# Dilated attention in a two-layer trunk: queries ordered by residue mod 4, two head groups in one contraction

## The chip, the cores and the metric

One Trainium2 chip, one of its cores. The metric is device time in microseconds for one execution of the whole program; smaller is better. TensorE is called PE here (PEld is its weight load), VectorE is DVE, ScalarE is ACT, GpSimd is POOL, and SP is the engine that issues most transfers.

## What is computed

Two layers over 256 tokens of width 1024, all in 32-bit floats. In each layer 24 heads of width 64 get q, k and v. Twelve of them are dilated heads, in three groups of four; six use plain causal softmax and six use stick-breaking attention. The part that matters:

```python
DIL_GROUPS = ((128, 1), (512, 4), (2048, 16))
# Query t attends to t, t-d, t-2d, ..., t-(window/d)*d. Returns (out, logsumexp)

def dilated_mixture(q, k, v):
    outs, lses = [], []
    for g, (w, d) in enumerate(DIL_GROUPS):
        sl = slice(g * HEADS_PER_DIL_GROUP, (g + 1) * HEADS_PER_DIL_GROUP)
        o, lse = dilated_window_attention(q[:, sl], k[:, sl], v[:, sl], w, d)
        outs.append(o)
        lses.append(lse)
    o = jnp.stack(outs, axis=0)
    wgt = jax.nn.softmax(jnp.stack(lses, axis=0), axis=0)
    return jnp.sum(wgt[..., None] * o, axis=0)
```

Weighting by the softmax of the log-sums is the same as one softmax over the keys of all three groups, and so the kernel computes it. With 256 tokens a query of group 1 meets keys at distances 0, 4, 8, ..., one of group 2 at 0, 16, 32, ...: in both cases only keys with its own residue mod 4, 64 of the 256. Around attention stand the projections (q, k, v, gates), the output projections with sigmoid gates, and a squared-ReLU MLP.

## The kernel before, in words

Activations lie with features on partitions and tokens along the free axis (`xres`, 128x8x256). Weights come in 280 pieces of 128x1024 (512 KB) in the order of use, through 4 buffers `raw`; SP issues every load (L109). Each piece is split by ACT (`wh`, L128) and DVE (`wl`, L129) into a high and a low part, in 6 buffers each, and a projection is three products per 128 rows (L211 to L213) of a 128x128 weight tile with 256 tokens. PE holds the weight tile, loaded by its own instruction before each product.

A layer begins with v for all heads (`v_chunk`, three chunks of 8 heads, L287), written out by `v_out` (L256) into `V[c]`, with tokens on partitions, as high and low parts. Then `MIX_ORDER` alternates q/k pairs (`qk_pair`, two heads each), gate tiles and attention units: `run_units` takes one or two units after each projection. A scheduler then orders the instructions of each engine by data dependence and priority, so that attention instructions stand between projection products in PE's queue.

`att_softmax(fs, kt_out, units)` does two dilated heads of each of the three groups (a "pair": `fs` names one q/k pair per group), twice per layer, four times in the program. `softmax_first` (L370) makes scores for the first 128 queries, `softmax_second` (L380) those for the other 128 against all 256 keys: 6 products of 64 rows (one head's width; the two heads j=0 and j=1 lie in the two halves of the rows) by 128 keys, and 6 by 256. `burst` (L312) keeps them together in PE's queue. The scores are plain 32-bit products, and each of them runs as two PE instructions (the trace has 192 of L319 for 96 in the program). `softmax_rows` (L349) adds the mask, takes the maximum, the exponential and the division, over 384 or 768 columns a head. `values(j)` (L409) then transposes the probabilities, three 128x128 tiles per group (L413 to L415), splits each result into `ph` and `pl`, and multiplies with V (`pv_mm`, L346 with both parts of V, 128 columns wide, and L347 with the high part, 64 wide). The same function with one group (G = 1) serves the six plain heads. `o_head` (L330) adds the two halves of the result.

Of the kernel before, what the change touches and what calls it, by code (L numbers as in the profile page):

```python
# [15 lines left out]
P = 128  # L16
# [28 lines left out]
NORM_ACT = False  # L45
TAIL = 4
# [17 lines left out]
def trunk(ctx: ExitStack, tc: tile.TileContext, w, x, norms, gfin, consts, out):  # L64
# [159 lines left out]

    hl = hilo_slot(0)
# [4 lines left out]
    for layer in range(DEPTH):  # L230
# [33 lines left out]

        def v_chunk(c, n):
# [23 lines left out]
            if c > 0:  # L289
                v_out(c)  # L290
# [21 lines left out]
        def burst(jobs, after=None):  # L312

            before = None
            with tc.high_priority(offset=BPRI):
                for dst, f, j, qs, ks, flipped, first in jobs:
                    t, own = QK[f], slice(j * DH, j * DH + DH)
                    q, k = t[own, 0, qs], t[own, 1, ks]
                    i = pe.matmul(dst, k if flipped else q, q if flipped else k, start=first, stop=True, skip_group_check=True)  # L319
                    if before is None and after is not None:  # L320
                        tc.add_manual_dep(i.ins, after.ins.name, READ, reason="the banks are free together")
                    if before is not None:
                        tc.add_manual_dep(i.ins, before.ins.name, QUEUED, reason="one burst of scores")
                    before = i

# [4 lines left out]
        def o_head(po, oF, j):  # L330

            tmp = T("tmp", [DH, S], 2)
            act.activation(tmp, po[DH:P, 0:S], AF.Copy)
            dve.tensor_tensor(oF[j * DH:(j + 1) * DH], po[0:DH, 0:S], tmp, op=ALU.add)
# [5 lines left out]
        def pv_mm(po, head, kt, ph, pl, first, last):  # L340

            c, s = divmod(head, 8)
# [19 lines left out]
        def att_softmax(fs, kt_out, units):  # L362

            G = len(fs)
            p0 = {}
            p1 = {}
            env = {}
            mA = cst["maskA"] if G == 3 else cst["maskB"].unsqueeze(1)

            def softmax_first():  # L370

                s0 = s_bank()
                t0 = T("wk", [P, 2, 3, P], WK)
                burst([(s0[:, j, g * P:(g + 1) * P], fs[g], j, T0, T0, False, True) for g in (2, 1, 0) for j in range(2)])
                for j in range(2):
                    env["read"] = softmax_rows(t0[:, j], s0[:, j, 0:384].rearrange("p (a b) -> p a b", a=3),
                                 mA[:, :, T1], env["den"][:, j:j + 1])
                    p0[j] = t0[:, j]

            def softmax_second():  # L380

                s1 = [s_bank().rearrange("p a b -> p (a b)") for _ in range(2)]
                burst([(s1[j][:, g * S:(g + 1) * S], fs[g], j, T1, TT, False, True) for g in (2, 1, 0) for j in range(2)], env["read"])
                for j in range(2):
                    t1 = T("wk", [P, 3, S], WK)
                    softmax_rows(t1, s1[j][:, 0:768].rearrange("p (a b) -> p a b", a=3), mA, env["den"][:, 2 + j:3 + j])
                    p1[j] = t1

            def softmax_one():
                s1 = s_bank()  # L390
                t1 = T("wk", [P, 2, 384], WK)
                burst([(s1[:, j, 0:S], fs[0], j, T1, TT, False, True) for j in range(2)]
                      + [(s1[:, j, S:384], fs[0], j, T0, T0, False, True) for j in range(2)])
                for j in range(2):
                    softmax_rows(t1[:, j, 0:S], s1[:, j, 0:S], cst["maskB"], env["den"][:, j:j + 1])
                    softmax_rows(t1[:, j, S:384], s1[:, j, S:384], cst["maskB"][:, T1], env["den"][:, 2 + j:3 + j])
                    p1[j] = t1[:, j:j + 1, 0:S]
                    p0[j] = t1[:, j:j + 1, S:384]

            def score():  # L400
                env["den"] = T("den", [P, 4], 3)
                if G == 3:
                    softmax_first()
                else:
                    softmax_one()
# [3 lines left out]
            def values(j):  # L409
                po = t_bank()  # L410
                for g in range(G):
                    tb = t_bank()
                    pe.transpose(tb[:, 0:P], p0[j][:, g], ident)  # L413
                    pe.transpose(tb[:, P:2 * P], p1[j][:, g, T0], ident)
                    pe.transpose(tb[:, 2 * P:3 * P], p1[j][:, g, T1], ident)  # L415
                    ph = T("ph", [P, 384], 2, F32R)
                    pl = T("pl", [P, 384], 2, F32R)
                    act.activation(ph, tb[:, 0:384], AF.Copy)
                    dve.tensor_tensor(pl, tb[:, 0:384], ph.bitcast(F32), op=ALU.subtract)
                    head = 2 * fs[g] + j  # L420
                    pv_mm(po, head, 0, ph[:, 0:S], pl[:, 0:S], g == 0, False)
                    pv_mm(po, head, 1, ph[:, S:384], pl[:, S:384], False, g == G - 1)
# [3 lines left out]

            units += [score] + [softmax_second] * (G == 3) + [lambda: values(0), lambda: values(1)]

# [350 lines left out]
```

## Time and profile before

| | us |
|---|---|
| median of 3 runs (869.42 to 870.21) | 870.13 |
| the profiled execution's own time | 869.13 |
| its span | 867.4 |
| PE busy | 855.4 (99%) |
| PEld busy | 780.6 (90%) |
| DVE busy | 638.3 (74%) |
| ACT busy | 475.5 (55%) |

Busy times overlap: a product's record reaches from its issue to its end and the next one starts inside it, so PE's 99% says that PE is hardly ever without work, and not how fast it works. What an instruction costs PE is read from the distance between the starts of neighbours. PE's granted clock is 0.999 over the span, that is 2.4 GHz throughout but for the start.

### The profile page before, as it was taken

What the parts mean: (1) busy time and instruction counts of PE and PEld (TensorE: products, weight loads), DVE (VectorE), ACT (ScalarE), POOL (GpSimd) and SP (SyncE); (2) the same over time, 40 slices, a digit from 0 to 9 for tenths busy, and PEclk for the clock granted to TensorE, in tenths of its full rate; (3) what the DMA queues carried; (4) which work ended last, traced back from release to release, by engine and by line L of the source; (5) the groups of instructions that cost most, each with busy time, mean ns of one, the idle gap of its engine ahead of it and who ended that gap; (6) DMA issues with size and microseconds to landing.
All of it is one profiled execution on the core that took longest, in us unless ns stands there. A gap on an engine that the chain in (4) does not pass through costs nothing.

```text
span 867.4 us, 14607 instructions
## 1 busy us (share of the span) xinstructions
PE 855.4 (99%) x5776; PEld 780.6 (90%) x5776; DVE 638.3 (74%) x962; ACT 475.5 (55%) x685; POOL 23.9 (3%) x36
## 2 busy tenths in 40 slices
PE   8999999999999999999999999999999999999996
PEld 6899999999998888888888999999999988888885
DVE  6978878855977766666578878798568977666664
ACT  6756666758454544444465665666574545444442
POOL 0000101000000000000000101010000000000000
PEclk9999999999999999999999999999999999999999
DMA  8854534454666565665555554435555675666641
GB/s 311 270 169 150 165 126 144 147 171 135 185 209 199 178 189 192 194 195 187 177 174 166 172 162 135 141 124 165 168 158 166 220 210 180 192 193 192 184 136 48
DMA packets 42835, 151.36 MB, mean 175 GB/s; under 512 B 4880, under 2 KB 5264, under 8 KB 42768
## 3 DMA queue, kind: packets, MB, share of 16 engines
q1 hardware_dynamic: 42336, 149.90, 54.8%
q8 instruction: 45, 0.74, 0.3%
q10 hardware_dynamic: 432, 0.54, 0.2%
q14 instruction: 22, 0.18, 0.1%
HBM read 149.37 MB, written 1.05 MB: 173 GB/s over the span
## 4 chain that ended last, share of the span: by engine, by line
PE 93%; DVE 2%; ACT 2%; issue 1%; DMA 1%; SPq 0%; POOLq 0%; DVEq 0%; ACTq 0%
PE mm L219 14%; PE mm L211 11%; PE mm L212 11%; PE mm L213 10%; PE mm L222 7%; PE s L603 7%; PE s L604 7%; PE s L605 7%; PE s L287 5%; PE s L319 2%; PE mm L287 2%; PE s L211 1%; PE t L346 1%; PE s L212 1%; PE s L213 1%
## 5 line engine op out<-in xcount | busy, mean ns | idle before, releaser
L129 DVE TENSOR_TENSOR wl<-raw,wh 128x1024 fp32r<-128x1024 f32 (+1 forms) x281 | 342.0, 1220 | 111.9 <-ACT wh L128 111.4
L128 ACT ACTIVATE wh<-raw 128x1024 fp32r<-128x1024 f32 (+1 forms) x281 | 294.8, 1053 | 221.2 <-PE mm L219 77.0
L211 PE MATMUL mm<-hl,wl 128*128 128x256 f32 x832 | 234.2, 282 | 0.0
L212 PE MATMUL mm<-hl,wh 128*128 128x256 f32 x832 | 233.1, 281 | 0.0
L213 PE MATMUL mm<-hl,wh 128*128 128x256 f32 x832 | 232.5, 280 | 0.6 <-DVE hl L242 0.4
L211 PEld LDWEIGHTS mm<-hl,wl 128*128 128x128 f32 x832 | 156.3, 188 | 0.8
L213 PEld LDWEIGHTS mm<-hl,wh 128*128 128x128 f32 x832 | 155.9, 188 | 1.0 <-DVE hl L242 1.0
L212 PEld LDWEIGHTS mm<-hl,wh 128*128 128x128 f32 x832 | 156.2, 188 | 0.3
L219 PE MATMUL mm<-hl,wh 128*128 128x512 f32 x512 | 129.1, 392 | 0.3 <-DVE wk L575 0.3
L219 PEld LDWEIGHTS mm<-hl,wh 128*128 128x128 f32 x512 | 93.7, 188 | 18.4 <-DVE wk L575 0.5
L603 PE MATMUL s<-wl,ga 128*128 128x512 f32 x256 | 100.4, 392 | 0.0
L604 PE MATMUL s<-wh,ga 128*128 128x512 f32 x256 | 100.0, 391 | 0.0
L605 PE MATMUL s<-wh,ga 128*128 128x512 f32 x256 | 99.0, 389 | 0.0
L222 PEld LDWEIGHTS mm<-hl,wl 128*128 128x128 f32 x512 | 70.4, 190 | 5.2
L575 DVE TENSOR_REDUCE wk<-mm 128x256 f32<-128x512 f32 x64 | 44.1, 691 | 41.4 <-PE mm L222 41.3
L222 PE MATMUL mm<-hl,wl 128*128 128x256 f32 x512 | 72.0, 282 | 0.0
L605 PEld LDWEIGHTS s<-wh,ga 128*128 128x128 f32 x256 | 48.0, 188 | 10.2
L603 PEld LDWEIGHTS s<-wl,ga 128*128 128x128 f32 x256 | 48.2, 188 | 9.9 <-ACT wk L668 0.5
L580 ACT ACTIVATE ga<-wk 128x512 fp32r<-128x512 f32 x32 | 20.2, 631 | 66.1 <-DVE wk L577 66.1
L604 PEld LDWEIGHTS s<-wh,ga 128*128 128x128 f32 x256 | 48.2, 188 | 8.8
L211 PE MATMUL s<-hl,wl 128*128 128x256 f32 x128 | 36.0, 281 | 0.6 <-DVE wk L531 0.6
L212 PE MATMUL s<-hl,wh 128*128 128x256 f32 x128 | 35.6, 278 | 0.0
(128 smaller groups left out, 1041.4 us busy)
## 6 DMA issues: line engine op xcount, KB each, us to landing
raw<-in_w_dram SPq DMA_DIRECT2D x279, 512.0 KB, 3.6
xres<-in_x_dram SPq DMA_DIRECT2D x4, 256.0 KB, 5.7
raw<-in_w_dram SPq DMA_DIRECT2D x2, 256.0 KB, 4.2
wk<-in_gfin_dram SPq DMA_DIRECT2D x2, 256.0 KB, 4.0
out_dram<-V SPq DMA_DIRECT2D x2, 256.0 KB, 2.3
out_dram<-V ACTq DMA_DIRECT2D x2, 256.0 KB, 2.1
c_maskA<-in_maskA_dram SPq DMA_DIRECT2D x1, 384.0 KB, 6.8
c_rope<-in_rope_dram SPq DMA_DIRECT2D x1, 256.0 KB, 6.6
```

Of the source, the lines that this page charges most:

```text
L128: act.activation(hi[:, c:c + step], r[:, c:c + step], AF.Copy)
L129: dve.tensor_tensor(lo[:, c:c + step], r[:, c:c + step], hi[:, c:c + step].bitcast(F32), op=ALU.subtract)
L211: pe.matmul(dst, lo[:, c:c + P], hl[:, koff + k, 0], start=a, stop=False, skip_group_check=True)
L212: pe.matmul(dst, hi[:, c:c + P], hl[:, koff + k, 0], start=False, stop=False, skip_group_check=True)
L213: pe.matmul(dst, hi[:, c:c + P], hl[:, koff + k, 1], start=False, stop=z, skip_group_check=True)
L219: pe.matmul(bank, hi[:, k * P:k * P + P], hl[:, k].rearrange("p a b -> p (a b)"), start=k == 0, stop=False, skip_group_check=True)
L222: pe.matmul(bank[:, 0:S], lo[:, k * P:k * P + P], hl[:, k, 0], start=False, stop=k == KT - 1, skip_group_check=True)
L287: last_mm = pe.matmul(pv[t], xs[:, k, x_part, t * P:t * P + P], w_part[:, wsl], start=k == 0 and w_part is hi and x_part == 0, stop=k == K ...
L575: dve.tensor_reduce(t[:, a], p[a].rearrange("p (a b) -> p b a", a=2), axis=mybir.AxisListType.X, op=ALU.add)
L603: pe.matmul(dst, uh[:, j % 2, k], lo[:, c], start=j == 0, stop=False)
L604: pe.matmul(dst, uh[:, j % 2, k], hi[:, c], start=False, stop=False)
L605: return pe.matmul(dst, ul[:, j % 2, k], hi[:, c], start=False, stop=j == 2 * npairs - 1)
```

## The change

The tokens of a query half are put on the score partitions by residue: partition r*32+i holds query 4i+r of the half. For the groups 1 and 2 a product then takes only the 32 queries and the 64 keys of one residue, and writes its own 32 partitions. Group 0 has the same order of queries, so it too is cut into four products of 32 queries, against 128 or 256 keys. Both halves become one softmax row layout of 256 or 384 columns a head (it was 384 or 768), with new masks. `att_softmax` is left for the plain heads.

For the contraction with V the probabilities of groups 1 and 2 lie side by side (64 + 64 columns), so one transpose serves both, and one product per residue contracts over 128 partitions: 64 keys of group 1 and 64 of group 2. V of those heads must lie that way, by residue: the chunks of v are reordered (`V_HEADS`) so that chunk 1 holds just these eight heads, and `v_out_dilated` writes it to four tiles `y` (in the buffers `ga`) and moves it by 16 transfers per layer, from SP, into `V[1]`.

```diff
+V_HEADS = list(range(0, 4)) + list(range(12, 16)) + list(range(4, 12)) + list(range(16, 24))
...
+        def v_out_dilated(c):
+
+            rcol, pv = factors["rcol"], banks[c]
+            V[c] = T("V", [P, DIL, 4, 2, DH], 3, F32R)
+            for t in range(2):
+                for g in range(2):
+                    p3 = pv[t][:, g * 256:g * 256 + 256].rearrange("p (a b) -> p a b", b=DH)
+                    y = T("ga", [P, 4, 2, DH], KT, F32R)
+                    act.activation(y[:, :, 0], p3, AF.Copy, scale=rcol[:, t:t + 1])
+                    dve.scalar_tensor_tensor(y[:, :, 1], p3, rcol[:, t:t + 1], y[:, :, 0].bitcast(F32), op0=ALU.mult, op1=ALU.subtract)
+                    to = g * SUB + t * SUB // 2
+                    for r in range(DIL):
+                        nc.sync.dma_start(V[c][to:to + SUB // 2, r].bitcast(F32), y[r:P:DIL].bitcast(F32))
...
+            def scores(h):
+
+                qs, ks, c = halves[h]
+                s = s_bank()
+                n = [0, P + c, P + c + SUB]
+                nq = P // DIL
+                jobs = [(fs[g], r, n[g], SUB) for g in (2, 1) for r in range(DIL)] + [(fs[0], r, 0, n[1]) for r in range(DIL)]
+                burst([(s[r * nq:(r + 1) * nq, j, c0:c0 + nk], by_residue(q_of(f, j, qs))[:, r],
+                        by_residue(k_of(f, j, TT))[:, r] if nk == SUB else k_of(f, j, ks), True)
+                       for f, r, c0, nk in jobs for j in range(2)])
...
+            def values(j):
...
+                pe.transpose(half(tb, 0), p0[j][:, T0], ident)
+                pe.transpose(half(tb, 1), p1[j][:, T0], ident)
+                pe.transpose(tb[:, S:384], p1[j][:, T1], ident)
...
+                pe.matmul(po[:, 0:S], v[:, 0].rearrange("p a b -> p (a b)"), ph[:, 0:S], start=True, stop=False, skip_group_check=True)
+                pe.matmul(po[0:DH, 0:S], v[:, 0, 0], pl[:, 0:S], start=False, stop=False, skip_group_check=True)
+                pe.matmul(half(po, 1), v[:, 1].rearrange("p a b -> p (a b)"), last[0], start=False, stop=False, skip_group_check=True)
+                pe.matmul(half(po[0:DH], 1), v[:, 1, 0], last[1], start=False, stop=False, skip_group_check=True)
+                tb = t_bank()
+                pe.transpose(half(tb, 0), p0[j][:, P:2 * P], ident)
+                pe.transpose(half(tb, 1), p1[j][:, 2 * P:3 * P], ident)
+                ph, pl = parts(tb, S)
+                for r in range(DIL):
+                    v = V[1][:, r, 2 * fs[0] + j]
+                    own = slice(r * SUB, r * SUB + SUB)
+                    pe.matmul(po[:, own], v.rearrange("p a b -> p (a b)"), ph[:, own], start=False, stop=False, skip_group_check=True)
+                    pe.matmul(po[0:DH, own], v[:, 0], pl[:, own], start=False, stop=r == DIL - 1, skip_group_check=True)
+                o_head(po, oF, j, lambda v: v.rearrange("p (r i) -> p i r", r=DIL))
```

How the rows stand in PE's queue, at the first pair of the first layer. Before, the first scores follow the values of a stick-breaking pair (`wk`, `V`), and the second scores (`s_878`, `s_879`, one bank a head) come 35 rows later, with projection products between:

```order
L347 MATMUL t_618<-wk_539,V_441 64x256
L346 MATMUL t_618<-wk_538,V_441 128x128
L347 MATMUL t_618<-wk_539,V_441 64x128
L319 MATMUL s_764<-qk_756 128x128 x2
L319 MATMUL s_764<-qk_689 128x128 x2
L319 MATMUL s_764<-qk_603 128x128 x2
...
L319 MATMUL s_878<-qk_756 128x256
L319 MATMUL s_879<-qk_756 128x256
L319 MATMUL s_878<-qk_689 128x256
L319 MATMUL s_879<-qk_689 128x256
L319 MATMUL s_878<-qk_603 128x256
L319 MATMUL s_879<-qk_603 128x256
```

With the change both halves stand in one run of 48 products, ahead of those values:

```order
L217 MATMUL mm_888<-hl_15_130,wh_752 128x256
L339 MATMUL s_788<-qk_780 32x64 x8
L339 MATMUL s_788<-qk_713 32x64 x8
L339 MATMUL s_788<-qk_627 32x128 x8
L339 MATMUL s_920<-qk_780 32x64 x8
L339 MATMUL s_920<-qk_713 32x64 x8
L339 MATMUL s_920<-qk_627 32x256 x8
L374 MATMUL t_634<-wk_562,V_465 128x256
```

Where there were two stretches of six products there is now one stretch of 48, so PE changes to the scores and back once a pair and not twice.

PE's values of the first head of that pair, groups 1 and 2 (`t_958` is the result, `V_363` the reordered chunk), with the change:

```order
L444 MATMUL t_971<-c_ident,wk_813 128x4x32
L445 MATMUL t_971<-c_ident,wk_945 128x4x32
...
L450 MATMUL t_958<-ph_974,V_363 128x64
...
L451 MATMUL t_958<-pl_975,V_363 64x64
L450 MATMUL t_958<-ph_974,V_363 128x64
L451 MATMUL t_958<-pl_975,V_363 64x64
L450 MATMUL t_958<-ph_974,V_363 128x64
L451 MATMUL t_958<-pl_975,V_363 64x64
L450 MATMUL t_958<-ph_974,V_363 128x64
L451 MATMUL t_958<-pl_975,V_363 64x64
```

Two transposes and eight products of 64 columns stand for six transposes and eight products of 256 and 128 columns before.

SP's queue in the first layer (`raw` are the weight loads):

```order
L113 DMA raw_501<-in_w_dram 128x1024
L285 DMA V_363<-ga_364 32x512 x2
L113 DMA raw_567<-in_w_dram 128x1024
L285 DMA V_363<-ga_364 32x512 x2
L113 DMA raw_597<-in_w_dram 128x1024
L285 DMA V_363<-ga_371 32x512 x3
L113 DMA raw_653<-in_w_dram 128x1024
L285 DMA V_363<-ga_371 32x512
L285 DMA V_363<-ga_378 32x512
L113 DMA raw_683<-in_w_dram 128x1024
L285 DMA V_363<-ga_378 32x512 x3
L113 DMA raw_720<-in_w_dram 128x1024
```

Before, the loads followed one another here. Now six of them stand behind transfers that wait for DVE to finish a tile `y`.

## Rows read from the trace of the kernel before

**Rows 1.** The page's part 1, PE: busy time, share of the span, instructions.
```profile
PE 855.4 (99%) x5776; PEld 780.6 (90%) x5776; DVE 638.3 (74%) x962; ACT 475.5 (55%) x685; POOL 23.9 (3%) x36
```
**Rows 2.** The page's part 4: shares of the chain that ended last.
```profile
PE 93%; DVE 2%; ACT 2%; issue 1%; DMA 1%; SPq 0%; POOLq 0%; DVEq 0%; ACTq 0%
```
**Rows 3.** Stretches: busy us of each engine from 60 to 150 us.
```profile
60.00:150.00 90.00, 90.00 (x775) 87.15 (x774) 73.86 (x128) 54.87 (x87) 8.53 (x12) 1.00 0.46 143
```
**Rows 4.** Timeline of PE around a pair's first scores: start us, us, what.
```profile
73.75 0.22 PE L346 MATMUL t<-wk,V 128*128 128x128 f32 x1
73.81 0.35 PE L347 MATMUL t<-wk,V 128*64 128x128 f32 x2
73.99 0.22 PE L346 MATMUL t<-wk,V 128*128 128x128 f32 x1
74.05 0.22 PE L347 MATMUL t<-wk,V 128*64 128x128 f32 x1
74.20 0.94 PE L319 MATMUL s<-qk 64*128 64x128 f32 x12
75.07 0.39 PE L211 MATMUL mm<-hl,wl 128*128 128x256 f32 x1
75.30 0.28 PE L212 MATMUL mm<-hl,wh 128*128 128x256 f32 x1
```
**Rows 5.** The same timeline around the second scores of that pair.
```profile
79.07 0.28 PE L211 MATMUL mm<-hl,wl 128*128 128x256 f32 x1
79.28 1.57 PE L319 MATMUL s<-qk 64*128 64x256 f32 x12
80.77 0.33 PE L413 MATMUL t<-c_ident,wk 128*128 128x128 f32 x1
80.86 0.36 PE L212 MATMUL mm<-hl,wh 128*128 128x256 f32 x1
81.06 0.28 PE L213 MATMUL mm<-hl,wh 128*128 128x256 f32 x1
```
**Rows 6.** The timeline of PE cut to 74.20 to 74.22 us.
```profile
74.20 0.38 PE L319 MATMUL s<-qk 64*128 64x128 f32 x2
```
**Rows 7.** The timeline of PE around two transposes of the values.
```profile
85.78 0.28 PE L211 MATMUL mm<-hl,wl 128*128 128x256 f32 x1
85.89 0.27 PE L414 MATMUL t<-c_ident,wk 128*128 128x128 f32 x1
86.00 0.27 PE L415 MATMUL t<-c_ident,wk 128*128 128x128 f32 x1
86.03 0.36 PE L212 MATMUL mm<-hl,wh 128*128 128x256 f32 x1
86.23 0.28 PE L213 MATMUL mm<-hl,wh 128*128 128x256 f32 x1
```
**Rows 8.** The timeline of PE, eight one-column products, each with a 128-wide weight load.
```profile
17.24 0.95 PE L188 MATMUL t<-ones,wk 128*128 128x1 f32 x8
```
**Rows 9.** Groups of DVE instructions by form: busy us, mean ns.
```profile
L263 DVE SCALAR_TENSOR_TENSOR V<-s,rc,V 128x512 fp32r<-128x512 f32 x8 | 6.0, 746 | 0.8 <-ACT V L262 0.8
L174 DVE SCALAR_TENSOR_TENSOR hl<-xres,c_norms,hl 128x256 fp32r<-128x256 f32 x32 | 13.9, 479 | 1.0 <-ACT hl L173 0.9
```
**Rows 10.** The timeline of PE where layer 1's v gives way to q and k.
```profile
471.33 0.28 PE L211 MATMUL mm<-hl,wl 128*128 128x256 f32 x1
471.45 0.28 PE L212 MATMUL mm<-hl,wh 128*128 128x256 f32 x1
472.14 0.38 PE L213 MATMUL mm<-hl,wh 128*128 128x256 f32 x1 [0.41 <-DVE hl L242]
```
**Rows 11.** Waits of SP's queue: us in total, times, longest.
```profile
SPq L109 <- DVE wl L129: 596.0, 226, 9.3
```
**Rows 12.** DMA from 20 to 60 us: the queue's share, then issues, KB, us to landing.
```profile
q1 hardware_dynamic: 2565, 9.34, 73.5%
...
raw<-in_w_dram SPq DMA_DIRECT2D x17, 512.0 KB, 4.5
```

More of the change, by code (lines that the diff above doesn't have):

```diff
@@ L45 @@
 NORM_ACT = False
+DIL = 4
+SUB = S // DIL
+V_HEADS = list(range(0, 4)) + list(range(12, 16)) + list(range(4, 12)) + list(range(16, 24))
 TAIL = 4
@@ L310, in qk_pair, with burst @@
             QK[f] = t
-        def burst(jobs, after=None):
+        def burst(jobs):
             before = None
             with tc.high_priority(offset=BPRI):
[L316 to L321, printed above, removed]
+                for dst, stationary, moving, first in jobs:
+                    i = pe.matmul(dst, stationary, moving, start=first, stop=True, skip_group_check=True)
                     if before is not None:
@@ L340, in pv_mm @@
         def pv_mm(po, head, kt, ph, pl, first, last):
-            c, s = divmod(head, 8)
+            c, s = divmod(V_HEADS.index(head), 8)
             dst = po[:, 0:S] if kt == 0 else po[:, P:S]
@@ L365, in att_softmax @@
+        def att_softmax(f, kt_out, units):
             p0 = {}
             p1 = {}
[L367 to L389, printed above, removed]
+            def score():
+                den = T("den", [P, 4], 3)
@@ L390, in softmax_one @@
                 s1 = s_bank()
                 t1 = T("wk", [P, 2, 384], WK)
-                burst([(s1[:, j, 0:S], fs[0], j, T1, TT, False, True) for j in range(2)]
-                      + [(s1[:, j, S:384], fs[0], j, T0, T0, False, True) for j in range(2)])
+                burst([(s1[:, j, 0:S], q_of(f, j, T1), k_of(f, j, TT), True) for j in range(2)]
+                      + [(s1[:, j, S:384], q_of(f, j, T0), k_of(f, j, T0), True) for j in range(2)])
                 for j in range(2):
[L395 to L398, printed above, removed]
@@ L409, in values @@
             def values(j):
[L410 to L422, printed above, removed]
+                po, tb = t_bank(), t_bank()
@@ new lines, in values @@
+                pe.transpose(tb[:, 0:P], p0[j], ident)
+                pe.transpose(tb[:, P:2 * P], p1[j][:, T0], ident)
+                pe.transpose(tb[:, 2 * P:3 * P], p1[j][:, T1], ident)
+                ph = T("ph", [P, 384], 2, F32R)
+                pl = T("pl", [P, 384], 2, F32R)
+                act.activation(ph, tb[:, 0:384], AF.Copy)
+                dve.tensor_tensor(pl, tb[:, 0:384], ph.bitcast(F32), op=ALU.subtract)
+                pv_mm(po, 2 * f + j, 0, ph[:, 0:S], pl[:, 0:S], True, False)
@@ L425, in values @@
                     o_split(oF, kt_out)
-            units += [score] + [softmax_second] * (G == 3) + [lambda: values(0), lambda: values(1)]
+            units += [score, lambda: values(0), lambda: values(1)]
         def att_c(i, units):
@@ L450, in logs @@
                 st = s_bank()
-                burst([(st[:, j, 0:S], f, j, TT, T0, True, True) for j in range(2)]
-                      + [(st[:, j, S:384], f, j, T1, T1, True, False) for j in range(2)])
+                burst([(st[:, j, 0:S], k_of(f, j, T0), q_of(f, j, TT), True) for j in range(2)]
+                      + [(st[:, j, S:384], k_of(f, j, T1), q_of(f, j, T1), False) for j in range(2)])
                 z = st[:, :, 0:384]
@@ L700, in constants @@
     dist = i[:, None] - i[None, :]
-    ok = [(dist >= 0) & (dist <= 128), (dist >= 0) & (dist % 4 == 0), (dist >= 0) & (dist % 16 == 0)]
-    m = [np.where(o, 0.0, NEG).astype(np.float32) for o in ok]
-    c["maskA"] = np.stack([a[P:] for a in m], axis=1)
+    half = []
+    for h in range(2):
+        p = np.arange(P)
+        r, own = p // (P // DIL), p % (P // DIL) + h * (P // DIL)
+        near = (DIL * own + r)[:, None] - np.arange((h + 1) * P)[None, :]
+        back = own[:, None] - np.arange(SUB)[None, :]
+        ok = [(near >= 0) & (near <= 128), back >= 0, (back >= 0) & (back % 4 == 0)]
+        half.append(np.concatenate([np.where(o, 0.0, NEG) for o in ok], axis=1))
+    c["maskA"] = np.concatenate(half, axis=1).astype(np.float32)
     c["maskB"] = np.where(dist >= 0, 0.0, NEG).astype(np.float32)[P:]
```

64 lines of the change are left out of this document (50 added, 14 removed).

## The prediction

> **What bounds the kernel.** I read the page's busy shares first, then the chain that ended last, then stretches, and last the timeline of PE around one pair. PE is busy 99% of the span [rows 1] and holds 93% of the chain; DVE and ACT have 2% each [rows 2]. From 60 to 150 us, where the first layer's attention lies, PE is busy in all of the 90 us, DVE in 73.9 and ACT in 54.9 [rows 3]. So attention work on DVE and ACT is covered by projection products, and the change is worth what it takes from or adds to PE's queue. Its smaller softmax (256 and 384 columns a head for 384 and 768) and fewer splits of probabilities lie on covered engines: I count them as nothing. Their cover is PE's queue; were it gone, they would be a gain, not a loss.
>
> How PE is paid for is read from starts. Ordinary projection products follow one another every 0.12 us (471.33 to 471.45) [rows 10]. A product of one column costs as much, 0.95/8 = 0.12 us: the next 128-wide weight load sets the pace there, not the columns [rows 8]. After a product of 128 columns the next starts 0.06 us later if its load is 64 wide (73.99 to 74.05) [rows 4]. So a distance is the longer of the columns streamed and the next load.
>
> **Transposes, removed.** Two transposes between projection products: without them L212 and L213 would start at 85.90 and 86.02; L213 starts at 86.23 [rows 7]. That is 0.21 us for two, 0.105 each. A pair had 2 heads x 3 groups x 3 = 18 and keeps 2 x 5 = 10, so 8 go per pair, 32 in the program: **-3.4 us**. All of it is on PE's path. Writing them in runs of 32 columns I count as nothing; at worst it doubles each of the 32 that are written so (8 per pair), +3.4 us, which nothing in the rows points to.
>
> **Values with V, changed.** For groups 1 and 2 of a head, two sets of four products (256, 256, 128, 128 columns, loads 128, 64, 128, 64 wide) go. By the distances above a set costs 0.12 + 0.12 + 0.06 + 0.06 (a transpose or a narrow load follows) = 0.36 us, so 4 x 0.36 = 1.44 us per pair go. In come four residues x two products of 64 columns, of which only the loads are felt: 0.06 + 0.12 = 0.18 us, 8 x 0.18 = 1.44 us per pair. **0 us**: a quarter of the columns, and the same time.
>
> **Scores, replaced.** This is the large term on both sides. First scores: after L347 at 74.05 the ordinary course would put L211 at 74.17 and L212 at 74.29; L212 starts at 75.30, so 1.01 us [rows 4]. Second scores: transpose, L212 and L213 would stand at 79.19, 79.30 and 79.42; L213 stands at 81.06, so 1.64 us [rows 5]. Together 2.65 us a pair. The two differ only in their columns: 6 products x 128 more columns cost 0.63 us, 0.82 ns a column, and 1.01 - 0.63 = 0.38 us is a fixed price of changing to the scores and back. The 0.82 ns already holds a doubling: two products (the two heads, in the two halves of PE's rows) start within 0.02 us [rows 6].
>
> With the change a pair has 48 products, 2 heads x 4 residues x (64 + 64 + 128 + 64 + 64 + 256) = 5120 columns for 2304 before, because group 0's keys are streamed once per residue. At 0.82 ns and one change of mode that is 4.20 + 0.38 = 4.58 us. But each product fills only 32 columns of PE's array, a strip of its own per residue, so strips may overlap as the row halves do. No row shows a product in a strip. The bounds: all four strips at once, 1.05 + 0.38 = 1.43 us; at the other end the pace of instructions. The 12 loads and 12 products of the first scores took 0.63 us beyond the fixed price, 26 ns an instruction, the fastest steady run in the rows; 192 instructions at 26 ns are 5.0 us, with the fixed price 5.4. I take the case next to what the rows show: each product is two PE instructions, the second must follow the first in its strip, and the next strip's first can run beside it. Two strips at a time make 2.10 + 0.38 = 2.48, and 0.1 for the two 32-wide loads that each 64-column product needs: 2.6 us. That is 4 x (2.6 - 2.65) = **-0.2 us**, between -4.9 and +11.
>
> The Trainium skill's page "TensorE: Matmul & The Clock Gate", Part 3, says that products in different column strips run concurrently, a few nanoseconds apart; [rows 6] agree for row halves, and strips no run here shows. By that rule the term would be the lower bound, -4.9 us.
>
> **v, changed.** Chunk 1 is written in 4 pieces of 256 columns instead of 2 of 512: DVE 4 x 479 = 1.92 us for 2 x 746 = 1.49 [rows 9], +0.4 us. In layer 1 PE waits 0.69 instead of 0.12 us for DVE where v gives way to q and k [rows 10], so I put **+0.4 us** there; in layer 0 no such wait stands, 0, at most another 0.4. The 16 transfers a layer stand in SP's queue, and the weight loads behind them wait for DVE's `y`. That queue has room: it waits 596 us for DVE to free `raw` [rows 11]. DMA is busy 73.5% of the 40 us in which layer 0's transfers fall, which moves 9.34 MB [rows 12]; 1 MB more would make it about 81%. Since a load lands in 4.5 us [rows 12] and several pieces lie split ahead, I count 0; the upper bound is half a landing per layer, 4.5 us in all.
>
> **Sum.** -3.4 + 0 - 0.2 + 0.4 = -3.2 us, against the profiled execution's 869.13: 865.9. The median before is 870.13, 1.0 us higher, so I forecast **866.9 us**.
>
> **Rivals.**
>
> *All strips at once.* For it: row halves do just this [rows 6], and eight products in a row go to eight different places. Against: it needs an instruction every 5.5 ns, where 26 ns is the fastest seen. It gives 4 x (1.43 - 2.65) = -4.9, in all -7.9: 862.2 us. Chance 0.15.
>
> *Slower: strips in single file.* If the queue lets a strip's product start only when the one before it in its row half is done, or if PE's instructions arrive too slowly, the burst costs 4.6 us or more. It decides the sign from 2.65 + 3.0/4 = 3.4 us a burst, because all other terms are worth -3.0. For it: three times the product instructions of an ordinary stretch, and 5120 columns for 2304. At 4.58 us: +7.7 - 3.0 = +4.7, 874.8 us; at 5.4 us 878. Chance 0.18.
>
> *Half pace for spaced operands.* The 64-column products read q and k every fourth float, 16 bytes apart, where all products in the rows read neighbours. If such a read goes at half the pace, the 2048 columns of these products cost, two strips at a time, 0.84 us more: 3.4 us a burst, +3.2 - 3.0 = +0.2, 870.3 us. An instruction pace of some 15 to 18 ns ends at the same place. Chance 0.20 together. The Trainium skill's page "SBUF — State Buffer", section "Door 1", speaks of 16-byte lines and a penalty for an access that goes to a new one; no row here shows it.
>
> *It doesn't do what it says:* the transposes go, but weight loads behind the transfers of V come late in both layers and PE waits for `wh` there, up to 4.5 us: 866.9 + 4 = 871 us. Against it: the slack in [rows 11]. Chance 0.05.
>
> **How the numbers follow.** The forecast has 0.42, the rivals 0.15, 0.18, 0.20 and 0.05. The range 862 to 875 us takes in the first rival and the plain single file; outside lie faster overlap than four strips and a slow instruction pace. The forecast's own range is 865 to 869. A measurement of this kernel tells 0.2%, 1.7 us, from no change. Faster by more (below 868.4): 0.15 and nine tenths of the forecast's 0.42, 0.52. Within it: the rest of the forecast and most of the third rival, 0.20. Slower: single file, the rest of the third and the late loads, 0.28.
>
> **What would show it.** In the profile after: transposes of the dilated heads 40 for 72; one stretch of scores a pair, and its length from the start before to the first ordinary distance after: 1.4, 2.6, 3.4 or 4.6 us tell the cases apart. How many score products start within 0.02 us tells how many strips overlap. The values' 64-column products should stand 0.06 and 0.12 us apart. Around 472 us PE's wait should be some 0.4 us longer, and no wait of PE for `wh` should appear near 25 to 40 and 460 to 480 us. The forecast is wrong if the stretch of scores is not near 2.6 us, or if PE gets waits that were not there.

## The result and the profile after

The changed kernel takes **864.12 us** (median of 6 runs, 863.97 to 865.5); the kernel before, on the same chip, 869.61 (868.82 to 870.21). The ratio is 0.994, with a 95% interval of 0.9927 to 0.9953: 5.5 us faster, where 3.2 were forecast. The profiled execution took 864.01 us, with a span of 862.3.

The page of the changed kernel, part 1, against [rows 1]:

```profile
PE 849.8 (99%) x6032; PEld 776.1 (90%) x6032; DVE 628.2 (73%) x958; ACT 468.2 (54%) x681; POOL 21.7 (3%) x36
```

PE has 256 products more than before and is done sooner; it still has work for 99% of the span. The shares of the chain are those of [rows 2] but for one point:

```profile
PE 93%; DVE 3%; ACT 2%; issue 1%; DMA 1%; SPq 0%; POOLq 0%; DVEq 0%; ACTq 0%
```

The stretch from 60 to 150 us, against [rows 3]: PE starts 932 products in the same 90 us instead of 775 and is never out of work, and DVE has 1.6 us less to do.

```profile
60.00:150.00 90.00, 90.00 (x932) 87.55 (x931) 72.26 (x142) 55.25 (x94) 7.64 (x12) 1.00 0.48 146
```

The timeline of PE around the first pair's scores, which answers to [rows 4] and [rows 5] together:

```profile
72.93 0.28 PE L217 MATMUL mm<-hl,wh 128*128 128x256 f32 x1
73.14 1.93 PE L339 MATMUL s<-qk 64*32 64x64 f32 x96
74.99 0.39 PE L374 MATMUL t<-wk,V 128*128 128x256 f32 x1
75.21 0.28 PE L375 MATMUL t<-wk,V 128*64 128x256 f32 x1
```

One stretch of 96 PE products (48 in the program, two each) stands where there were two. Read as in the prediction: L374 and L375 would stand at 73.05 and 73.17 in the ordinary course, L375 stands at 75.21, so the scores of a pair cost **2.04 us**, for 2.65 before and 2.6 forecast. The other three pairs agree within 0.06 us. The same timeline cut to 73.13 to 73.19 us tells how many strips overlap:

```profile
73.14 0.36 PE L339 MATMUL s<-qk 64*32 64x64 f32 x8
```

Eight products start within 0.05 us: two row halves times four strips. [Rows 6] had two.

The values' 64-column products, on the timeline of PE:

```profile
88.15 0.28 PE L450 MATMUL t<-ph,V 128*128 128x64 f32 x1
88.26 0.22 PE L451 MATMUL t<-pl,V 128*64 128x64 f32 x1
88.32 0.28 PE L450 MATMUL t<-ph,V 128*128 128x64 f32 x1
```

They stand 0.11 and 0.06 us apart, as forecast. Where layer 1's v gives way to q and k, PE's timeline has, for [rows 10]:

```profile
468.30 0.28 PE L216 MATMUL mm<-hl,wh 128*128 128x256 f32 x1
469.32 0.38 PE L217 MATMUL mm<-hl,wh 128*128 128x256 f32 x1 [0.74 <-DVE hl L250]
```

A distance of 1.02 us stands where 0.69 was: +0.33. DMA between 20 and 60 us, the queue's share and the new transfers, against [rows 12]:

```profile
q1 hardware_dynamic: 3268, 10.18, 83.0%
...
V<-ga SPq DMA_DIRECT2D x16, 64.0 KB, 5.4
```

DMA is busier (83.0% for 73.5%; 81% was forecast). The weight loads of this stretch still land in 4.5 us, and PE has the same two waits for `wh` as before, both before 10 us and so ahead of these transfers.

One difference between the traces lies where nothing was edited, and it moves comparisons of a microsecond. In the output projections of layer 1 the same products, in the same number, run at two paces. Busy time of each engine in 20 us there, before the change and after it, and in the kernel below that loads V once for both parts:

```profile
646.00:666.00 20.00, 20.00 (x179) 20.00 (x178) 19.52 (x35) 8.36 (x13) 0.00 (x0) 1.00 0.71 213
640.00:660.00 20.00, 20.00 (x172) 20.00 (x172) 19.20 (x34) 8.48 (x14) 0.00 (x0) 1.00 0.66 211
638.50:658.50 20.00, 20.00 (x179) 20.00 (x178) 19.52 (x35) 8.67 (x14) 0.00 (x0) 1.00 0.71 211
```

PE is busy throughout, and the granted clock is 1.00 in all three, but 179 products start in one stretch and 172 in the other: 0.114 or 0.118 us from start to start. Over 240 products there (from 638.65 us on in the changed kernel) this makes 0.94 us, to the changed kernel's loss. The cause is open. The 15 runs of the kernel before that were made beside the second group of experiments fall into four from 869.03 to 869.25 us and eleven from 869.75 to 870.52, as if some executions had that pace and others not; one execution of each kernel was traced, so this is not shown. Where a microsecond matters below, the traces are therefore also followed from one projection product to the same one in the other trace, and only through the attention of the two layers (in the trace before 62 to 225 us and 472 to 622 us). There the changed kernel takes 3.13 and 3.17 us less than the kernel before. (The granted clock of the kernel before is lower at the very end, 0.56 from 865 to 867.4 us, when PE has no work left, and not at the start, as said above.)

### The profile page after: what moved, and what is told of

Read it like the earlier page. It is cut to its first block, busy times and chain, and to the rows that moved or that the text cites. A ratio compares the mean times of both kernels' runs of the same rounds, so it can differ in the third digit from the quotient of the medians.

```text
span 862.3 us, 15138 instructions
## 1 busy us (share of the span) xinstructions
PE 849.8 (99%) x6032; PEld 776.1 (90%) x6032; DVE 628.2 (73%) x958; ACT 468.2 (54%) x681; POOL 21.7 (3%) x36
## 3 DMA queue, kind: packets, MB, share of 16 engines
HBM read 149.31 MB, written 1.05 MB: 174 GB/s over the span
## 4 chain that ended last, share of the span: by engine, by line
PE 93%; DVE 3%; ACT 2%; issue 1%; DMA 1%; SPq 0%; POOLq 0%; DVEq 0%; ACTq 0%
PE mm L223 14%; PE mm L215 11%; PE mm L217 11%; PE mm L216 11%; PE mm L226 7%; PE s L668 7%; PE s L669 7%; PE s L670 7%; PE s L309 5%; PE s L339 2%; PE mm L309 2%; PE s L215 1%; PE s L217 1%; PE s L216 1%; PE t L215 1%
```

## The experiments

The score stretch was the term that came out differently, so most runs are about it. Three theories could set its pace of 0.12 us for eight 64-column products: the weight loads, the rate at which PE's instructions arrive, or the spacing of the operands (every fourth float, 16 bytes apart). The first five runs do 16 products of each half once more, at the head of that half's scores, so that a pair has 160 PE products instead of 96, and vary what the repeated ones read. Their output is overwritten by the products that follow. One execution of each was timed and traced; what counts is the length of the stretch in its trace.

### Repeated as they are

```diff
+                twice = [(s[r * nq:r * nq + nq, j, n[g]:n[g] + SUB], by_residue(q_of(f, j, qs))[:, r], by_residue(k_of(f, j, TT))[:, r], True)
+                         for g in (2, 1) for r in range(DIL) for f in (fs[g],) for j in range(2)]
+                burst(twice + [...
```

> Each of the eight score bursts halves is preceded by a copy of its 16 products of 64 columns (written to the same place and then overwritten by the real ones). In the changed kernel eight such products (one in each strip of each row half) take a slot of about 0.125 us, twice per set because each product is two PE instructions. All theories: 4 slots a half more, +0.50 us a half, +1.0 us a burst, +4.0 us in the program; a burst of 3.0 us instead of 2.0. If the copies overlapped with the rest and cost less, the slot would not be what paces a burst.

868.47 us. The timeline of PE of this kernel:

```profile
73.24 2.92 PE L339 MATMUL s<-qk 64*32 64x64 f32 x160
76.09 0.39 PE L374 MATMUL t<-wk,V 128*128 128x256 f32 x1
```

From the first product to L374 it is 2.85 us, for 1.85 in the changed kernel (73.14 to 74.99): +1.00 us for 64 products, 0.125 for each eight. The rest of the group is read against that.

### Repeated with neighbours

```diff
-  by_residue(q_of(f, j, qs))[:, r], by_residue(k_of(f, j, TT))[:, r]
+  q_of(f, j, slice(qs.start + r * nq, qs.start + (r + 1) * nq)), k_of(f, j, slice(r * SUB, (r + 1) * SUB))
```

> The same 16 extra products a half, but reading 32 neighbouring queries and 64 neighbouring keys instead of every fourth. Theory loads (the four 32-wide weight loads of a row half follow one another, about 30 ns each, 4 x 30 = 0.12 us a slot): no difference from the plain copies, +1.0 us a burst. Theory instructions (a slot's 32 instructions arrive at 4 ns each, or 16 pairs at 8 ns): no difference either. Theory spacing (operands 16 bytes apart are read at half the pace, 0.107 us a slot instead of 0.054): the extra slots fall to about 0.06 us, +0.5 us a burst, half of the plain copies.

868.32 us. The stretch, on the timeline of PE:

```profile
73.98 2.63 PE L339 MATMUL s<-qk 64*32 64x64 f32 x160
76.55 0.39 PE L374 MATMUL t<-wk,V 128*128 128x256 f32 x1
```

It is 2.57 us, +0.72. Clearer than the sum is the timeline cut to the first 0.25 us of the stretch, in which only repeated products run. First the kernel with the products repeated as they are, then this one:

```profile
73.24 0.48 PE L339 MATMUL s<-qk 64*32 64x64 f32 x16
```

```profile
73.98 0.46 PE L339 MATMUL s<-qk 64*32 64x64 f32 x32
```

Twice as many products start in the same time, with the same number of loads and of columns. For these first 32 products that speaks for the spacing and against the other two. (Eight products are 16 PE instructions with their loads, not the 32 of the expectation.)

### Only the keys neighbours

```diff
-  by_residue(k_of(f, j, TT))[:, r]
+  k_of(f, j, slice(r * SUB, (r + 1) * SUB))
```

> Sixteen 64-column products are done once more at the head of each half's scores, as in the run with repeated products; the repeated ones read their queries (the weight load) every fourth float and their keys (the streamed columns) as neighbours. If it is the streamed operand that goes at half pace when its floats stand 16 bytes apart, eight of the repeated products take 0.06 to 0.07 us, as with neighbours for both. If it is the weight load, 0.12 us.

867.66 us. The timeline cut to 73.12 to 73.38 us, the first 0.25 us after the first start:

```profile
73.12 0.47 PE L339 MATMUL s<-qk 64*32 64x64 f32 x28
```

28 products with spaced queries and neighbouring keys, for 32 and 16: it is the streamed operand that pays for its spacing. After the first eight, which took 0.11 us, eight products take 0.062 us here as well.

### Loads of 16 columns instead of 32

```diff
-  s[r * nq:r * nq + nq, ...], by_residue(q_of(f, j, qs))[:, r]
+  s[r * nq:r * nq + 16, ...], by_residue(q_of(f, j, qs))[:, r, 0:16]
```

> The same extra products with every fourth query and key as in the change, but with 16 queries a load instead of 32 (the same number of instructions and columns). Theory loads: the four loads of a row half take 4 x 15 = 0.06 us, the extra slots fall to about 0.06 us, +0.5 us a burst. Theory spacing of the keys and theory instructions: 0.125 us a slot as in the plain copies, +1.0 us a burst.

867.67 us; the stretch is +0.94 (73.04 to 75.83). The first 0.25 us:

```profile
73.04 0.54 PE L339 MATMUL s<-qk 64*16 64x64 f32 x20
```

Halving the load brings next to nothing: with spaced keys, loads don't set the pace.

### 32 columns instead of 64

```diff
-  n[g]:n[g] + SUB], ..., by_residue(k_of(f, j, TT))[:, r]
+  n[g]:n[g] + 32], ..., by_residue(k_of(f, j, TT))[:, r, 0:32]
```

> The same extra products against 32 keys instead of 64 (the same loads, the same number of instructions, half the columns). Theory loads and theory instructions: 0.125 us a slot, +1.0 us a burst, as the plain copies. Theory spacing of the keys: a slot of half the length, about 0.06 us, +0.5 us a burst.

867.43 us; the stretch is +0.74 (73.11 to 75.70). The first 0.25 us:

```profile
73.11 0.48 PE L339 MATMUL s<-qk 64*32 64x32 f32 x31
```

Half of the spaced columns start at twice the rate, and stand level with 64 neighbouring ones. So a spaced column takes about twice the time of a neighbouring one. That both kernels, this one and the one with neighbours, end at +0.72 to +0.74 and not at twice 0.27 shows that something else takes over further into the stretch.

### The order of the strips

```diff
-  jobs = [(fs[g], r, n[g], SUB) for g in (2, 1) for r in range(DIL)] + [(fs[0], r, 0, n[1]) for r in range(DIL)]
+  jobs = [(fs[g], r, n[g], SUB if g else n[1]) for r in range(DIL) for g in (2, 1, 0)]
```

> The same 48 score products of a half pair, but all those of one strip (one residue) stand together in PE's queue: three of each row half, then the next strip. Theory overlap by neighbours (PE takes products from its queue in order, and a product waits behind the one before it only if both need the same strip of the same row half): now only the two row halves can run side by side, so a pair's stretch takes as long as single file of the strips, 4.4 to 4.6 us for 2.04, and the time grows by 4 x 2.4 to 2.6 = +10 us, to about 874. Rival, the strips never overlap but the array is quicker with 32 columns than I reckoned: the order of the strips is of no matter, the stretch stays at 2.0 us and the time at 864. Second rival, the stretch is paced by the number of PE instructions: no change either.

868.5 us (10 runs, 867.68 to 868.91), ratio to the kernel before 0.9984 (0.9975 to 0.9993). PE's timeline:

```profile
72.79 0.28 PE L217 MATMUL mm<-hl,wh 128*128 128x256 f32 x1
73.00 3.06 PE L339 MATMUL s<-qk 64*32 64x64 f32 x96
75.99 0.39 PE L374 MATMUL t<-wk,V 128*128 128x256 f32 x1
76.22 0.28 PE L375 MATMUL t<-wk,V 128*64 128x256 f32 x1
```

A pair costs 76.22 - 73.03 = 3.19 us, 1.15 more than with the strips in turn, 4.6 us over four pairs; the time grew by 4.4. So the overlap of strips is real and is worth 4 to 5 us, and both rivals fall. But the theory's size falls too: it said 4.4 to 4.6 us. A group of PE's products by form, from 73.00 to 73.48 us and then from 73.00 to 73.60, shows why:

```profile
L339 PE MATMUL s<-qk 64*32 64x64 f32 x12 | 0.7, 299 | 0.0
...
L339 PE MATMUL s<-qk 64*32 64x64 f32 x16 | 0.8, 300 | 0.0
L339 PE MATMUL s<-qk 64*32 64x128 f32 x2 | 0.3, 288 | 0.0
```

In PE's queue 8 products of 64 columns (four in the program) are followed by 4 of 128, all of the first strip, and then come the second strip's. Yet 12 of 64 columns start before the first of 128. The second strip's products do not wait for those of the first strip that stand before them in the queue.

### Two stretches instead of one

The first product of the second half loses its high priority, and an empty unit stands before it; the rest follows it.

```diff
+            for n, (dst, stationary, moving, first) in enumerate(jobs):
+                with tc.high_priority(offset=0 if n < later else BPRI):
...
+            units += [first, lambda: None, lambda: scores(1), lambda: values(0), lambda: values(1)]
```

> The same 48 score products of a pair, but the 24 of the second query half stand some 30 rows later in PE's queue, with projection products between, so that PE changes to the scores and back twice a pair, as before the change. Theory fixed price: my forecast took 0.38 us for one change to the scores and back, out of the difference between products of 128 and 256 columns; the time then grows by 4 x 0.38 = 1.5 us, to about 865.6. Rival, the 0.38 us were no price of the change of mode but time of the products themselves (a start that does not overlap): no growth beyond 0.2 us a pair, 864.1 to 864.9.

867.94 us (11 runs, 866.98 to 868.49), ratio 0.9976 (0.9967 to 0.9985). PE's timeline:

```profile
72.74 0.28 PE L217 MATMUL mm<-hl,wh 128*128 128x256 f32 x1
72.95 1.00 PE L339 MATMUL s<-qk 64*32 64x64 f32 x48
...
74.10 0.28 PE L375 MATMUL t<-wk,V 128*64 128x256 f32 x1
...
77.14 0.28 PE L217 MATMUL mm<-hl,wh 128*128 128x256 f32 x1
77.35 1.21 PE L339 MATMUL s<-qk 64*32 64x64 f32 x48
...
78.72 0.28 PE L216 MATMUL mm<-hl,wh 128*128 128x256 f32 x1
```

The first stretch costs 74.10 - 72.98 = 1.12 us, the second 78.72 - 77.38 = 1.34: 2.46 for 2.04. The fixed price of a change to the scores and back is therefore 0.42 us; the forecast had 0.38. Over four pairs that is 1.7 us, but the time grew by 3.8. Followed through the attention of both layers, this kernel takes 1.9 us more than the changed one, so the fixed price explains nearly all of it there. The other 2.0 us lie behind it, in the output projections of layer 1, where 7 more of PE's products stand and the waits are longer. The longest on the timeline:

```profile
647.16 0.28 PE L217 MATMUL s<-hl,wh 128*128 128x256 f32 x1
648.10 0.39 PE L215 MATMUL s<-hl,wl 128*128 128x256 f32 x1 [0.66 <-DVE wk L596]
```

The changed kernel waits 0.30 us for the same line of DVE, at 638.65. The rest was not traced to its places. Moving a unit moved work behind it, and here that was not free.

### Transposes done twice

```diff
                 pe.transpose(half(tb, 0), p0[j][:, T0], ident)
                 pe.transpose(half(tb, 1), p1[j][:, T0], ident)
+                pe.transpose(half(tb, 0), p0[j][:, T0], ident)
+                pe.transpose(half(tb, 1), p1[j][:, T0], ident)
```

and so for the other two of a head.

> The four transposes of a dilated head whose result is written in runs of 32 columns are done twice (32 more in the program, the same result written again). My forecast took 0.105 us for a transpose and nothing for the runs: +3.4 us over the changed kernel, about 867.5. Rival, writing in runs of 32 columns halves a transpose's pace, so that each costs about 0.2 us: +6.4 us, about 870.5. Second rival, a transpose hides behind its neighbours' weight loads and costs under 0.06 us: less than +2 us, about 866.

866.57 us (5 runs, 866.06 to 868.03), ratio 0.9965 (0.9952 to 0.9977): +2.45 us, 0.077 for each of 32. On the timeline of PE:

```profile
84.89 0.29 PE L446 MATMUL t<-c_ident,wk 128*128 128x128 f32 x1
85.01 0.27 PE L447 MATMUL t<-c_ident,wk 128*128 128x128 f32 x1
85.12 0.27 PE L448 MATMUL t<-c_ident,wk 128*128 128x128 f32 x1
85.23 0.27 PE L449 MATMUL t<-c_ident,wk 128*128 128x128 f32 x1
```

They stand 0.11 to 0.12 us apart, written in runs of 32 columns, as those of [rows 7] written in one piece. The half pace falls. The time grew by 1 us less than 32 x 0.11 because this trace has the pace of 0.114 us in the output projections of layer 1, and the changed kernel's has not: through the attention of both layers it takes 3.2 us more, 0.10 for each transpose.

### No transfers

```diff
+                p3 = pv[t].rearrange("p (a b) -> p a b", b=DH)
+                to = V[c].rearrange("p r a c b -> p (r a) c b")[:, 8 * t:8 * t + 8]
+                act.activation(to[:, :, 0], p3, AF.Copy, scale=rcol[:, t:t + 1])
+                dve.scalar_tensor_tensor(to[:, :, 1], p3, ...)
```

These lines stand for the loops over `g` and `r` and their transfers.

> V of the dilated heads is written straight into its tile in two pieces, as before the change: no tiles y and none of the 32 transfers, so the reordering of V by residue is left out and the values of groups 1 and 2 are multiplied with V rows in token order. Theory: the transfers cost nothing, and only the two extra pieces on DVE show, as PE's wait where layer 1's v gives way to q and k: -0.3 us against the changed kernel, within 0.2%. Rival, weight loads behind the transfers come late: up to 4.5 us are gained, and PE's waits for wh in 25 to 40 and 460 to 480 us go away.

863.73 us (5 runs, 862.5 to 863.89), ratio 0.9927 (0.9914 to 0.9939): 0.4 us less than the changed kernel, which the intervals cannot tell from nothing, and far from 4.5. PE's timeline at the end of layer 1's v:

```profile
468.12 0.28 PE L216 MATMUL mm<-hl,wh 128*128 128x256 f32 x1
468.81 0.39 PE L217 MATMUL mm<-hl,wh 128*128 128x256 f32 x1 [0.41 <-DVE hl L250]
```

The distance is back at 0.69 us, the value of [rows 10]. Followed from projection product to projection product, this trace gains 0.35 us at this place, 0.24 before 15 us (ahead of all transfers), and between and behind them the difference ends up where it was to within 0.1. So the 0.33 us belong to the four pieces on DVE, and the transfers cost nothing that can be measured.

### Stored by residue

If spaced keys cost twice, q and k of groups 1 and 2 can be stored in order of residue. The last addition of the rotation writes them so, in two halves, from a buffer between.

```diff
+                    for a in range(2):
+                        dve.tensor_tensor(t[:, a].rearrange("p (r i) -> p r i", r=DIL), by_residue(mixed[:, a]), by_residue(sh[:, a]), op=ALU.add)
...
+                        q_of(f, j, slice(r * SUB + h * nq, r * SUB + (h + 1) * nq)) if nk == SUB else by_residue(q_of(f, j, qs))[:, r],
+                        k_of(f, j, slice(r * SUB, (r + 1) * SUB)) if nk == SUB else k_of(f, j, ks), True)
```

> q and k of groups 1 and 2 are stored in order of residue (the last addition of the rotation on DVE writes them so, from a buffer between), so that all 64-column score products read neighbours. Theory half pace for spaced operands: eight of these products then take 0.06 instead of 0.125 us, 8 slots of them in a pair, so a pair's stretch falls from 2.04 us by 0.35 to 0.5 us and the time by 1.4 to 2 us, to about 862.5; less if the instructions' own pace (about 0.095 us for sixteen, as the second half of the run with neighbours showed) takes over, then -1 us. Rival, weight loads or instructions set the pace: the stretch and the time stay as they are, 864. The extra work on DVE (one addition cut in two) is covered by PE.

863.52 us (5 runs, 863.47 to 864.04), ratio 0.9929 (0.9916 to 0.9941). PE's timeline:

```profile
73.25 0.28 PE L215 MATMUL mm<-hl,wl 128*128 128x256 f32 x1
73.46 1.68 PE L346 MATMUL s<-qk 64*32 64x64 f32 x96
75.08 0.38 PE L381 MATMUL t<-wk,V 128*128 128x256 f32 x1
75.30 0.28 PE L382 MATMUL t<-wk,V 128*64 128x256 f32 x1
```

A pair costs 75.30 - 73.49 = 1.81 us, 0.23 less, 0.9 over four pairs. The theory holds, with the smaller gain that it put beside the first, and in the time no more than 0.6 us arrive, which the intervals don't separate from the changed kernel (0.4 through the attention of both layers; where the other 0.5 goes was not found). Why the stretch itself gains less than twice the pace is seen in the starts of every eighth product of the stretch (ns after the first, from the trace; the last number is the start of the next projection or values product):

```
                     four x 64 columns    two x 128   four x 64             two x 256
changed kernel       0  131  258  378     495  624    735  844  962  1089   1209  1449   1855
stored by residue    0   80  136  191     266  431    573  666  721   861    939  1189   1614
```

The first four groups go from 0.124 to 0.067 us each. The 128-column groups behind them, which were not changed, go from 0.12 up to 0.15, and the second four reach only 0.092. Something other than columns sets the pace once the products come that fast. The runs with repeated products meet it too: in their second half the repeated eights take 0.095 us each with neighbours and 0.094 with 32 spaced columns, so whatever the columns, eight products behind the first 32 need some 0.09 us. They have the same 16 instructions and the same 32-wide loads in all three, so an instruction pace (about 6 ns each, an estimate from these eights) and the loads are both left as its cause; no run tells them apart.

### One V load for both parts, and both together

High and low parts of the probabilities lie side by side, and one product with one load streams both.

```diff
-                    pe.matmul(po[:, own], v..., ph[:, own], ...)
-                    pe.matmul(po[0:DH, own], v[:, 0], pl[:, own], ...)
+                    pe.matmul(two[:, :, own], v.rearrange("p a b -> p (a b)"), pp[:, :, own], start=False, stop=r == DIL - 1, skip_group_check=True)
```

> The high and low parts of the probabilities lie side by side in one tile, so that the values of a dilated head take one V load and one product over both parts instead of two: 4 products of 128 columns for 8 of 64 in groups 1 and 2, three of 512, 128 and 128 columns for four in group 0; the extra V columns that come out for the low part are left unread but one more addition on DVE is needed. Theory, a 64-column product is paid for by its 128-wide load (0.11 us before the first of the two, 0.06 after it): a residue takes 0.11 to 0.12 us instead of 0.17, 0.2 us a head saved there, and group 0 costs about the same (512 columns at the pace of two times 256): 8 x 0.2 = 1.6 us less, about 862.5. Rival, the wider product waits longer for DVE's low part than the narrow one did, which only moves it behind projection products: no gain, 864.

861.76 us (4 runs, 861.57 to 862.63), ratio 0.9909 (0.9895 to 0.9922): 2.4 us less than the changed kernel. PE's timeline of one head's values:

```profile
84.35 0.39 PE L438 MATMUL t<-pp,V 128*128 128x512 f32 x1
84.58 0.34 PE L440 MATMUL t<-pp,V 128*128 128x128 f32 x2
84.75 0.30 PE L443 MATMUL t<-c_ident,wk 128*128 128x128 f32 x1
...
88.41 0.56 PE L449 MATMUL t<-pp,V 128*128 128x128 f32 x4
88.81 0.29 PE L433 MATMUL t<-c_ident,wk 128*128 128x128 f32 x1
```

0.40 us for group 0 and 0.40 for the four residues; the changed kernel takes 0.12 + 0.12 + 0.06 + 0.06 and 4 x 0.17, so 1.04 becomes 0.80, 1.9 us over eight heads. Through the attention of both layers the trace gives 1.6 us, as forecast; 0.9 of the 2.4 us come from the pace of the output projections, which in this trace is the 0.114 us. With both edits:

> Both together: q and k of groups 1 and 2 stored by residue, and one V load for both parts. The two gains are in different stretches of PE's queue and should add up: 0.6 us (measured for the first) and 1.6 us (forecast for the second) less than the changed kernel, about 861.9 us. Rival, PE waits for DVE where the extra additions stand: not below 863.5.

861.4 us (4 runs, 860.88 to 862.07), ratio 0.9903 (0.989 to 0.9917). It has the lowest median of all, but only 0.4 us below the one-load kernel alone, and their intervals overlap. The two traces differ in that pace, though: this one has 0.118 us. Through the attention of both layers it takes 0.84 us less than the one-load kernel and 2.4 less than the changed one. So the traces show both gains, in the size that the distances gave (0.9 and 1.6); the times alone do not show the first.

## Why the prediction was right, and where it was off

The sign and the range held. By its own sign of being wrong, a stretch of scores that is not near 2.6 us, the forecast failed in that term, and 864.12 us lies below its own 865 to 869. Of the miss of 2.8 us, 0.5 is the median before (869.61 here, 870.13 there), 2.2 the scores and 0.1 v.

- **Transposes, -3.4 us: right as far as it was tested.** Forty are left of 72; at 0.11 us from start to start and none slower for its runs of 32 columns. The 32 repeated ones cost 3.2 us through the attention of both layers, for 3.4 forecast.
- **Values, 0: right.** The 64-column products stand 0.11 and 0.06 us apart, and their loads, not their columns, are what is paid for: one load for both parts, with the same columns, takes 1.6 us away.
- **v, +0.4: right.** 0.33 us at the named place, gone when the pieces are whole again. Layer 0 shows no such wait.
- **Transfers, 0: right.** They are there, they land in 5.4 us, and without them nothing is gained.
- **Scores, -0.2: mis-sized; measured 4 x (2.04 - 2.65) = -2.4 us.** The step that failed is "Two strips at a time make 2.10 + 0.38 = 2.48, and 0.1 for the two 32-wide loads". Its parts went three ways. The fixed price holds (0.42 for 0.38). The strips overlap not two but four at a time, which makes 1.05 + 0.38 = 1.43 us. The spaced keys go at half pace, which I had as a rival by itself; with four strips side by side 2048 more columns at 0.82 ns would cost 0.42 us and make 1.85. Measured, storing by residue takes only 0.23 of that away and leaves 1.81, so of the 0.61 us above 1.43 the spacing is shown for 0.23, and 0.38 stay with the pace behind the first 32 products, whose cause is open. The two loads for which I added 0.1 us hardly show: with those of the repeated products halved, the stretch is 0.06 us shorter. So two rivals were both true, one against the other, and between them the result came out near my figure for reasons that were not mine: what I took for one lane too few was in part an operand read too slowly.

The sum by measured terms is -3.4 + 0 - 2.4 + 0.3 = -5.5 us, and the medians differ by 5.5. That agreement is in part chance. The two profiled executions differ by 5.1: the attention of both layers takes 6.3 us less, of which the terms name 5.8 and 0.5 has no name, v of layer 1 takes 0.3 more, and the slower pace in the output projections 0.9 more, for which the prediction had no term.

My ground against four strips was that they need an instruction every 5.5 ns, where 26 ns was the fastest in the rows. That figure was no bound: those 24 instructions were held up by their columns, as the difference between 128 and 256 columns could have told me. A rate seen where something else sets the pace says nothing of what an engine can do. The rule of the Trainium skill's page "TensorE: Matmul & The Clock Gate", Part 3, on strips that run side by side stands: eight start within 0.05 us. The same part of that page of the Trainium skill says that products start strictly in the order of the program; the run with the strips one behind the other shows 64-column products starting ahead of 128-column ones that precede them (12 before the first of 128, where 8 stand before it), so for different strips the trace decides otherwise. What the Trainium skill's page "SBUF — State Buffer", section "Door 1: The DMA port swizzle", says of 16-byte lines, that an access which goes to a new line pays for it, agrees with the streamed operand (16 products for 32 in 0.25 us); for the loaded operand hardly any such price shows (28 for 32).

## What to carry to other kernels

When products fill only part of the array, put different strips and row halves next to one another in the queue, and price them as running side by side: here their order alone was worth 4.4 us. Look at how the streamed operand lies before cutting columns: a quarter of the columns at a step of four floats is worth only half of what it seems. And where columns are few, count loads: one load that serves two streams brought more than the fewer columns did.

## What was not expected of the hardware

- Products of different strips overtake one another in PE's queue: 12 of 64 columns started where 8 and then 4 of 128 stand in the program.
- A 32-bit streamed operand at a step of 16 bytes goes at half pace (eight products of 64 columns: 0.125 us for 0.063 to 0.067); the loaded operand at the same step shows hardly any such price (28 products for 32 in 0.25 us).
- Once products start at less than 0.07 us for eight, products behind them slow down (0.12 to 0.15 us for eight of 128 columns), and later eights of 64 columns take 0.09 us and not 0.06; the cause is open.
- The same run of projection products, at the same granted clock and with PE busy throughout, has 0.114 us from start to start in some traces and 0.118 in others, 0.94 us over 240 products. Two kernels a microsecond apart need their traces compared before the difference is put down to the edit.
- DVE, too, is slow where it reads by residue. Its additions of the kernel that stores by residue, in a group by form, take 640 ns for 256 columns, where the changed kernel's take 718 for 512:

```profile
L331 DVE TENSOR_TENSOR qk<-sh,sh 128x256 f32<-128x256 f32 x16 | 9.7, 640 | 0.1
L328 DVE TENSOR_TENSOR qk<-qk,sh 128x512 f32<-128x512 f32 x18 | 12.9, 718 | 0.2
```
